# Seven-product FFN blocks: two partial sums copied into PSUM by ScalarE, products in the order 1 5 6 2 7 3 4, weight operands rounded two at a time

## The chip, the cores and the metric

The kernel runs on one core of a Trainium2 chip. The metric is the device time of one execution in microseconds (us), the median of several runs. The core's engines are TensorE (PE in the profile; PEld is its weight load), VectorE (DVE), ScalarE (ACT), GpSimd (POOL) and SyncE (SP, which issues the DMA transfers here). Each engine runs its own queue of instructions in order; semaphores tie the queues together. SBUF is the on-chip memory of 128 partitions; PSUM is the memory into which TensorE accumulates, in banks of 128 x 512 float32.

## The reference

One layer of a hybrid backbone over 512 latent tokens and 128 context tokens, 640 in all: a modulated RMSNorm, a mixer (attention beside a short convolution), a gated residual, and then the feed-forward network (FFN), which is the part that matters here:

```python
h2 = _rms(x, norm_ffn) * (1 + sc2) + sh2
gate, up = jnp.split(h2 @ w_gate_up, 2, axis=-1)      # 1024 -> 2 x 2816
x = x + g2 * ((jax.nn.silu(gate) * up) @ w_down)      # 2816 -> 1024
```

Everything is float32. The kernel gets float32 accuracy out of TensorE by splitting each operand into a rounded high part and a low part, and by three matmuls for each product (high by high, high by low, low by high).

## The kernel before, in words

**Phases.** The mixer takes the first part of the span. From about 318 us on the kernel computes the FFN. Its 2816 columns are cut into 22 blocks f of 128, in four groups (`GCUT` = 0, 6, 12, 17, 22). After each group, `down` multiplies the finished blocks by their rows of `w_down` and adds into the residual.

**A block.** For block f the operands are the columns of gate (raw tile g, 1024 x 128, two halves A11 and A12 of the 1024 rows) and of up (raw tile u, halves A21 and A22); on the token side they are B11, B12, B21, B22, the two halves of the 1024 features by two halves of the 640 tokens (`LO`, `HI`, 320 each). Blocks 0 and 1 (`NPLAIN` = 2) do the eight half products plainly (`plain`). Blocks 2 to 21 use seven products in place of eight, in the manner of Strassen and Winograd: sums S1 to S4 of the weight halves (VectorE, `op_load` L190 on, the sums at L206) and sums T1 to T4 of the token quarters, computed once (`b_sums` L1060 and L1073). One product (`prod`) is four steps of 128 rows, each with three matmuls of 128 x 320 (`mm3`, L154 to L157): twelve matmuls.

**Products and what joins them.** TensorE's queue is written out by hand, in this order for a block before: P1 = A11 B11 into bank b1 (`ff_a`); P5 = S1 T1 into b3 (`ff_c`); the end of the block before (`ff_end`: VectorE and ScalarE only); P6 = S2 T2 onto b1 (`ff_d`); P2 = A12 B21 into b2 (`ff_b`); and in `ff_e` P7 = S3 T3 onto b1, P4 = A22 T4 into b4, P3 = S4 B22 onto b3. Between them ScalarE copies b1 to SBUF three times (`copy_of` L1187, the copy itself at L1191), as p1 after P1, u2 after P6 and u3 after P7, since the next product goes on adding into the same bank. VectorE adds: b2 + p1 (L1204), then ScalarE's SiLU (L1205); b3 + u3 into cu HI (L1220), which reads b3 before P3 goes on into it; b4 + u3 into cu LO and the product with the SiLU; and in `ff_end` b3 + u2, SiLU (L1231), product (L1232). `ff_out` splits the result into gT, 128 x 640, high part on ScalarE and low part on VectorE.

**Weights.** SP issues the loads (L224), 512 KB for each raw tile, into a ring of three raw tiles (`WFB` = 3). A raw tile is free again when the last sum or rounding that reads it is done. `split` (L150 to L152) makes a rounded operand: ScalarE copies the source into the high part, VectorE subtracts that from the source for the low part. Before, each half (A11, S1, S2, A12, S3, A22, S4) is one such operand of 128 x 512, and its high and low part share one tile; the tiles `wh` and `wl`, four of each, are used in turn. `W` and `plan` keep a list of loads and operands and issue them ahead of their use, `AOP` entries ahead for the FFN.

**What sets the order.** VectorE and ScalarE get their instructions by a scheduler with priorities: `early(n)` raises what it encloses (`SOP` for the operands, `CPP` for the copies, `GSP` for gT's split). While blocks 0 and 1 run, VectorE's order is written out by hand as well, with the low parts of the first weights, the token sums and then the weights of block 2. PSUM in the FFN has six banks for the products and for `down` and two for the rest.

Of the kernel before, what the change touches and what calls it, by code (L numbers as in the profile page):

```python
# [9 lines left out]
F32 = mybir.dt.float32  # L10
F32R = mybir.dt.float32r
AF = mybir.ActivationFunctionType
ALU = mybir.AluOpType
AX = mybir.AxisListType

P = 128
# [4 lines left out]
TOK = NT * P  # L21
# [7 lines left out]
HALF = TOK // 2  # L29
# [23 lines left out]
CPP = 50  # L53
GSP = 30
FEND = 2
AOP = 9
NPLAIN = 2
PPO = ''
RSP = 0
# [4 lines left out]
SPO = 0  # L64
# [18 lines left out]
WHB = 4  # L83
# [8 lines left out]
def build(ctx, tc, x_prompt, x_sample, c, cache_k, cache_v, c_ctx, norm_mix, norm_ffn, w_ada, b_ada,  # L92
# [3 lines left out]
    act, dve, pool, pe, sp = nc.scalar, nc.vector, nc.gpsimd, nc.tensor, nc.sync  # L96
# [4 lines left out]
    def open_pool(name, side, names):  # L101
        g = tc.tile_pool(name=name, bufs=1, side=side, reuse_waits="tile")
        pools[name] = (g, g.__enter__())
        for n in names.split():
            where[n] = name
# [14 lines left out]
    def T(tag, shape, dt=F32, bufs=1):  # L120
        seq[0] += 1
        return pools[where.get(tag, "A")][1].tile(list(shape), dt, tag=tag, bufs=bufs, name=f"{tag}_{seq[0]}")

    def PB(shape=(P, 512), dt=F32, tag="t"):
        seq[0] += 1
        if kept.get(tag):
            w = kept[tag].pop()
            n = 1
            for y in shape[1:]:
                n *= y  # L130
            w = w[:, :n] if tag != "s" else w
            if tag != "s" and len(shape) > 2:
                names = "abc"[:len(shape) - 1]
                w = w.rearrange("p (" + " ".join(names) + ") -> p " + " ".join(names), **dict(zip(names, shape[1:])))
            return w
        return pools["psum"][1].tile(list(shape), dt, tag=tag, bufs=pbufs[tag], name=f"p{tag}_{seq[0]}")
# [7 lines left out]
    def f32(ap):  # L144
        return ap.bitcast(F32)

    def early(n):
        return tc.high_priority(n)

    def split(hi, lo, src):  # L150
        act.activation(hi, src, AF.Copy)  # L151
        dve.tensor_tensor(lo, src, f32(hi), ALU.subtract)  # L152

    def mm3(out, lh, ll, rh, rl, start, stop, more=False):  # L154
        pe.matmul(out, lh, rh, start=start, stop=False, skip_group_check=more)  # L155
        pe.matmul(out, lh, rl, start=False, stop=False, skip_group_check=more)  # L156
        pe.matmul(out, ll, rh, start=False, stop=stop, skip_group_check=more)  # L157
# [34 lines left out]
    ops = [0]  # L192

    def op_load(e):

        f, name = e[0][1:]
        g, u = (order[place[x, f]][5] for x in "gu")
        a11, a12, a21, a22 = g[:, 0:4], g[:, 4:8], u[:, 0:4], u[:, 4:8]
        if name[0] == "S":
            if name == "S1":  # L200
                sums[f] = T("sx", (P, 2, 4, P), F32, 2)
            s13, s24 = sums[f][:, 0], sums[f][:, 1]
            src, x, y, op = {"S1": (s13, a21, a22, ALU.add), "S2": (s24, s13, a11, ALU.subtract),
                             "S3": (s13, a11, a21, ALU.subtract), "S4": (s24, a12, s24, ALU.subtract)}[name]
            with early(SOP[f >= NPLAIN]):
                (pool if f < SPO else dve).tensor_tensor(src, x, y, op)  # L206
        else:
            src = {"A11": a11, "A12": a12, "A21": a21, "A22": a22}[name]
        w = T(("wh", "wl")[ops[0] % 2], (P, 2, 4, P), F32R, WHB)
        ops[0] += 1  # L210
        with early(SOP[f >= NPLAIN]):
            split(w[:, 0], w[:, 1], src)
        e[5] = w

    sums = {}

# [34 lines left out]
    def load_next(later=False):  # L251
        load(order[stream_at[0]], later)
        stream_at[0] += 1

    def W(key):
        p = place[key]
        while not in_pre[0] and stream_at[0] < len(order):
            nxt = order[stream_at[0]][0][0]
            ahead = AO if nxt == "o" else AOP if nxt in ("g", "u", "op") else AHEAD
            if stream_at[0] > p + ahead or order[stream_at[0]][2] > phase[0]:  # L260
                break
            load_next()
        assert order[p][5] is not None, key
        return order[p][5]
# [19 lines left out]
            plan(("ada", 5, j, kp), wa[:, 2 * kp:2 * kp + 2, 5 * D + j * 512:5 * D + (j + 1) * 512], 2, "f")  # L284

    GROUPS = [list(range(a, b)) for a, b in zip(GCUT, GCUT[1:])]
    PLAIN, PRODS = ("A11", "A12", "A21", "A22"), ("A11", "S1", "S2", "A12", "S3", "A22", "S4")

    def plan_raw(f, x, ph=3):
        col = f * P + (DFF if x == "u" else 0)  # L290
# [297 lines left out]
    for x in P1SEQ.split():  # L588
        k = int(x[1:] if x[0] == "d" else x[1:2] or 0)
# [306 lines left out]
    cu = {}  # L896
# [89 lines left out]
    LO, HI = slice(0, HALF), slice(HALF, TOK)  # L986
# [55 lines left out]
    B = {}  # L1042
# [35 lines left out]
    for j in range(2):  # L1078
        cols = slice(j * 512, (j + 1) * 512)
        for n, t in enumerate(TORD):  # L1080
# [8 lines left out]
            for half in range(2):  # L1089
                for p in range(4):  # L1090
                    wh, wl = W(("o", j, 2 * half + p // 2))
# [22 lines left out]
            with early(XP[j]):  # L1114
                m = T("mix", (P, 512), F32, 2)
                if j == 0:
                    act.activation(m, ab[0], AF.Copy, scale=rA[t])
                    dve.scalar_tensor_tensor(m, ab[1], rB[t], m, ALU.mult, ALU.add)
                    e = pool if n < PX else dve
# [28 lines left out]
    close_pool("D")  # L1148
    close_pool("F")
    open_pool("Y2", "left", "B22 T1 T2 T3 T4")  # L1150
    open_pool("G", "right", "cg cu p1 u2 u3 dm tr")
    gT, st, pair = {}, {}, [None]

    def FB():
        return PB((P, 512), tag="f")

    def prod(out, f, a, b, start=True, stop=True, more=False):
        w = W(("op", f, a))
        for k in range(4):
            mm3(out[:, :HALF], w[:, 0, k], w[:, 1, k], *B[b][k], start and k == 0, stop and k == 3, more)  # L1160

    def plain(f, bs, toks, mid=None):

# [24 lines left out]
    def copy_of(tag, ps):  # L1188
        x = T(tag, (P, HALF))
        with early(CPP):  # L1190
            act.activation(x, ps[:, :HALF], AF.Copy)  # L1191
        return x

    def ff_a(f):
        b1 = FB()
        prod(b1, f, "A11", "B11")
        cg = T("cg", (P, TOK), F32, 2)
        st[f] = [b1, copy_of("p1", b1), cg, None, None, None, None]

    def ff_b(f):  # L1200
        b2 = FB()
        prod(b2, f, "A12", "B21")
        b1, p1, cg = st[f][0:3]
        dve.tensor_tensor(cg[:, LO], b2[:, :HALF], p1, ALU.add)  # L1204
        act.activation(cg[:, LO], cg[:, LO], AF.Silu)  # L1205

    def ff_c(f):
        st[f][3] = FB()
        prod(st[f][3], f, "S1", "T1")

    def ff_d(f):
        prod(st[f][0], f, "S2", "T2", start=False, more=True)
        st[f][4] = copy_of("u2", st[f][0])

    def ff_e(f):
        b1, _, cg, b3, u2 = st[f][0:5]
        prod(b1, f, "S3", "T3", start=False, more=True)
        u3 = copy_of("u3", b1)
        cu = T("cu", (P, TOK), F32, 2)
        dve.tensor_tensor(cu[:, HI], b3[:, :HALF], u3, ALU.add)  # L1220
        b4 = FB()
        prod(b4, f, "A22", "T4")
        dve.tensor_tensor(cu[:, LO], b4[:, :HALF], u3, ALU.add)
        dve.tensor_tensor(cu[:, LO], cu[:, LO], cg[:, LO], ALU.mult)
        prod(b3, f, "S4", "B22", start=False, more=True)
        st[f] = cg, cu, b3, u2

    def ff_end(f):
# [46 lines left out]
    for gi, grp in enumerate(GROUPS):  # L1275
        for f in grp:
            if f == 0:
                dve_order = tc.manual_schedule(engines={mybir.EngineType.DVE})
                dve_order.__enter__()
                b_plain("B12 B22", slice(0, 192))  # L1280
                for x in range(NPLAIN):
                    plain(x, ("B11", "B21"), LO, None if x else lambda: h2_turn(TORD[-1], BPL))
                    if x == 0:
                        with early(BPL):
                            b_plain("B12 B22", slice(192, HALF))
                        b_sums(slice(128, HALF))
                        for _ in range(4):
                            load_next()
                b_sums(slice(0, 128))
                dve_order.__exit__(None, None, None)  # L1290
                phase[0] = 3
                for x in range(NPLAIN):
                    plain(x, ("B12", "B22"), HI)
            elif f >= NPLAIN:
                ff_a(f)
                if f - 1 in st and FEND == 1:
                    ff_end(f - 1)
                ff_c(f)
                if f - 1 in st:
                    ff_end(f - 1)  # L1300
                ff_d(f)
                ff_b(f)
                ff_e(f)
                if f == grp[-1] or FEND == 0:
                    ff_end(f)
# [6 lines left out]


tile_hymba = with_exitstack(build)

_INS = ["x_prompt", "x_sample", "c", "cache_k", "cache_v", "c_ctx", "norm_mix", "norm_ffn", "w_ada", "b_ada",
# [44 lines left out]
```

## Time and profile before

| | |
|---|---|
| timed runs | 757.63, 758.66, 758.73 us; median 758.66 us |
| profiled execution, its span | 755.2 us; no other time is shown for it, and the median of the runs is 3.5 us above this span |
| TensorE busy | 737.5 us, 98% of the span, 4618 matmuls |
| VectorE busy | 551.7 us, 73% |
| ScalarE busy | 378.8 us, 50% |
| DMA | 84.52 MB, mean 112 GB/s |
| granted TensorE clock | 0.999 |

The span runs from the first to the last recorded instruction of one profiled execution; the timed runs are other executions. A line of the timeline is: start in us, length in us, engine, line of the kernel, operation, output tile <- input tiles (buffer numbers left out), shapes, count, and in brackets how long the engine stood idle before it and what it waited for. Instructions on one engine overlap a little at their ends, so what an instruction costs its engine is read from start to start.

### The profile page before, as it was taken

The page shows a single profiled execution, that of the slowest core. Times are in us where ns is not written, and L with a number is a line of the kernel's source. Part 1 is how long each engine was busy: PE and PEld are TensorE (multiplying, and loading weights), DVE is VectorE, ACT ScalarE, POOL GpSimd, SP SyncE. Part 2 cuts the span into 40 slices and gives each one's busy share as a digit, 9 for nine tenths or more (in the row PEclk, how much of TensorE's full clock was granted, in tenths as well). Part 3 has the DMA queues.
Part 4 walks back from the last instruction along what each step waited for, and adds up shares of the span by engine and source line. Part 5 has one row for each costly group of instructions (what it writes and reads, how often), then busy time and mean ns, then how long its engine had stood idle before and what let it go on. Part 6 is the DMA issues. An engine that isn't in the chain of part 4 may idle for free.

```text
span 755.2 us, 11953 instructions
## 1 busy us (share of the span) xinstructions
PE 737.5 (98%) x4618; PEld 665.2 (88%) x4618; DVE 551.7 (73%) x997; ACT 378.8 (50%) x745; POOL 42.6 (6%) x75
## 2 busy tenths in 40 slices
PE   7999899999999999999999999999999999999997
PEld 5678888988998887899998799998889998899986
DVE  5558877666666798779979778884678866788653
ACT  5356777667656534765552235553125541255410
POOL 2403101011000110100000000000000000000000
PEclk9999999999999999999999999999999999999999
DMA  9985133532432464031235313133113232222312
GB/s 290 294 236 163 51 104 102 165 92 91 159 107 91 133 224 138 1 112 54 81 118 157 108 58 110 58 111 112 56 56 104 67 112 78 62 86 84 112 56 83
DMA packets 101389, 84.52 MB, mean 112 GB/s; under 512 B 3502, under 2 KB 81650, under 8 KB 101332
## 3 DMA queue, kind: packets, MB, share of 16 engines
q1 hardware_dynamic: 100980, 83.39, 35.9%
q8 instruction: 36, 0.59, 0.3%
q0 software_dynamic: 352, 0.37, 0.3%
q14 instruction: 21, 0.17, 0.1%
HBM read 79.68 MB, written 2.75 MB: 109 GB/s over the span
## 4 chain that ended last, share of the span: by engine, by line
PE 83%; DVE 7%; ACT 5%; DMA 2%; issue 1%; SPq 1%; POOL 0%; ACTq 0%
PE pf L155 17%; PE pf L157 17%; PE pf L156 17%; PE pc L710 3%; PE pc L712 3%; PE pc L711 3%; PE po L868 3%; PE ps L824 2%; PE ph L155 2%; PE ph L157 2%; PE ph L156 2%; PE pc L388 2%; PE pt L851 2%; DMA wf<-in_w_in_dram 1%; PE ps L155 1%
## 5 line engine op out<-in xcount | busy, mean ns | idle before, releaser
L151 ACT ACTIVATE wh<-wf 128x512 fp32r<-128x512 f32 (+1 forms) x68 | 55.5, 816 | 81.1 <-PE pf L157 59.3
L155 PE MATMUL pf<-wh,gT 128*128 128x512 f32 (+1 forms) x225 | 86.9, 386 | 0.0
L156 PE MATMUL pf<-wl,gT 128*128 128x512 f32 (+1 forms) x225 | 86.5, 385 | 0.0
L157 PE MATMUL pf<-wh,gT 128*128 128x512 f32 (+1 forms) x225 | 86.5, 384 | 0.0
L710 PE MATMUL pc<-hH,wh 128*128 128x320 f32 x192 | 61.1, 318 | 0.0
L712 PE MATMUL pc<-hH,wl 128*128 128x320 f32 x192 | 59.3, 309 | 0.0
L711 PE MATMUL pc<-hL,wh 128*128 128x320 f32 x192 | 59.3, 309 | 0.0
L152 DVE TENSOR_TENSOR wl<-wf,wh 128x1024 fp32r<-128x1024 f32 (+1 forms) x34 | 39.4, 1160 | 25.2 <-ACT wh L151 22.1
L155 PE MATMUL pf<-T,wh 128*128 128x320 f32 x160 | 49.6, 310 | 0.5 <-ACT u L1191 0.5
L156 PEld LDWEIGHTS pf<-wl,gT 128*128 128x128 f32 x225 | 42.3, 188 | 8.6 <-issue 0.2
L155 PEld LDWEIGHTS pf<-wh,gT 128*128 128x128 f32 x225 | 42.3, 188 | 8.6 <-issue 0.2
L157 PEld LDWEIGHTS pf<-wh,gT 128*128 128x128 f32 x225 | 42.3, 188 | 8.3
L156 PE MATMUL pf<-T,wh 128*128 128x320 f32 x160 | 49.4, 309 | 0.0
L155 PE MATMUL pf<-T,wl 128*128 128x320 f32 x160 | 49.4, 309 | 0.0
L156 PE MATMUL pf<-T,wl 128*128 128x320 f32 x160 | 49.4, 309 | 0.0
L157 PE MATMUL pf<-T,wl 128*128 128x320 f32 x160 | 49.4, 309 | 0.0
L157 PE MATMUL pf<-T,wh 128*128 128x320 f32 x160 | 49.4, 309 | 0.0
L155 PE MATMUL pf<-B,wl 128*128 128x320 f32 x152 | 47.1, 310 | 0.0
L157 PE MATMUL pf<-B,wl 128*128 128x320 f32 x152 | 47.0, 309 | 0.0
L156 PE MATMUL pf<-B,wl 128*128 128x320 f32 x152 | 47.0, 309 | 0.0
L155 PE MATMUL pf<-B,wh 128*128 128x320 f32 x136 | 42.2, 310 | 1.5 <-DVE cu L1220 1.5
L151 ACT ACTIVATE wl<-wf 128x512 fp32r<-128x512 f32 x34 | 21.2, 625 | 41.6 <-PE pf L156 34.8
(306 smaller groups left out, 2058.7 us busy)
## 6 DMA issues: line engine op xcount, KB each, us to landing
wf<-in_w_gate_up_dram SPq DMA_DIRECT2D x44, 512.0 KB, 4.0
aw<-in_w_ada_dram SPq DMA_DIRECT2D x24, 512.0 KB, 4.1
wf<-in_w_down_dram SPq DMA_DIRECT2D x20, 512.0 KB, 3.3
wf<-in_w_in_dram SPq DMA_DIRECT2D x18, 512.0 KB, 5.5
af<-in_w_ada_dram SPq DMA_DIRECT2D x32, 256.0 KB, 6.4
x<-in_x_sample_dram SPq DMA_DIRECT2D x8, 512.0 KB, 6.2
wf<-in_w_out_dram SPq DMA_DIRECT2D x8, 512.0 KB, 4.4
wf<-in_w_ada_dram SPq DMA_DIRECT2D x8, 512.0 KB, 3.7
```

The lines of the kernel that those rows point to most:

```text
L151: act.activation(hi, src, AF.Copy)
L152: dve.tensor_tensor(lo, src, f32(hi), ALU.subtract)
L155: pe.matmul(out, lh, rh, start=start, stop=False, skip_group_check=more)
L156: pe.matmul(out, lh, rl, start=False, stop=False, skip_group_check=more)
L157: pe.matmul(out, ll, rh, start=False, stop=stop, skip_group_check=more)
L388: pe.matmul(out[CG * g:CG * (g + 1)], cp[:, k], w, start=(k < 4), stop=(k >= KD - 4), skip_group_check=True)
L710: pe.matmul(acc, wh[:, k], hH[k][:, c0:c0 + n], start=(k == 0), stop=False)
L711: pe.matmul(acc, wh[:, k], hL[k][:, c0:c0 + n], start=False, stop=False)
L712: pe.matmul(acc, wl[:, k], hH[k][:, c0:c0 + n], start=False, stop=(k == KD - 1))
L824: pe.matmul(s2[:, g, :320], q, kk[:, v, P + g * 320:P + (g + 1) * 320], start=(i == 0), stop=(i == 1))
L851: pe.transpose(tp[:, i, h], u[3][h][:, kt * P:(kt + 1) * P], ident)
L868: pe.matmul(ov, w, x[:, i].rearrange("p a q -> p (a q)"), start=(g == 0 and i == 0 and n == 0), stop=(last and i == len(kts) - 1 and n == 1))
```

## The change

In the blocks of seven products, three things are different.

- After P1 ScalarE copies b1 into the PSUM bank b2, and P2 accumulates on it; after P7 it copies b1 into the bank b4, and P4 accumulates on that. The copies p1 and u3 in SBUF, and the two additions on VectorE that used them for the `LO` half, are gone. SiLU reads b2, and the product for cu LO reads b4 straight from PSUM.
- The last three products run as P7, P3, P4 in place of P7, P4, P3. A new copy p5 of b3 is taken to SBUF after P5; cu HI is then b1 + p5 and no longer reads b3.
- Operands are rounded two at a time: A11 with A12, A21 with A22 in the plain blocks, S1 with S2, S3 with S4; one tile `wh` of 128 x 1024 is the high part of both, one tile `wl` the low part. A22 of the seven-product blocks is still rounded alone. `AOP` is 6 in place of 9.

```diff
-AOP = 9
+AOP = 6
@@ op_load
-            if name == "S1":
-                sums[f] = T("sx", (P, 2, 4, P), F32, 2)
-            s13, s24 = sums[f][:, 0], sums[f][:, 1]
-            src, x, y, op = {"S1": (s13, a21, a22, ALU.add), "S2": (s24, s13, a11, ALU.subtract),
-                             "S3": (s13, a11, a21, ALU.subtract), "S4": (s24, a12, s24, ALU.subtract)}[name]
+            if name == "S12":
+                sums[f] = T("sx", (P, 8, P), F32, 2)
+            s13, s24 = sums[f][:, 0:4], sums[f][:, 4:8]
             with early(SOP[f >= NPLAIN]):
-                (pool if f < SPO else dve).tensor_tensor(src, x, y, op)
+                for out, x, y, op in {"S12": ((s13, a21, a22, ALU.add), (s24, s13, a11, ALU.subtract)),
+                                      "S34": ((s13, a11, a21, ALU.subtract), (s24, a12, s24, ALU.subtract))}[name]:
+                    dve.tensor_tensor(out, x, y, op)
+            src = sums[f]
         else:
-            src = {"A11": a11, "A12": a12, "A21": a21, "A22": a22}[name]
-        w = T(("wh", "wl")[ops[0] % 2], (P, 2, 4, P), F32R, WHB)
-        ops[0] += 1
+            src = {"A1": g, "A2": u, "A22": a22}[name]
+        if name == "A22":
+            w = T(("wh", "wl")[ops[0] % 2], (P, 2, 4, P), F32R, WHB)
+            ops[0] += 1
+            e[5] = w[:, 0], w[:, 1]
+        else:
+            e[5] = T("wh", (P, 8, P), F32R, WHB), T("wl", (P, 8, P), F32R, WHB)
         with early(SOP[f >= NPLAIN]):
-            split(w[:, 0], w[:, 1], src)
-        e[5] = w
+            split(*e[5], src)
...
-    PLAIN, PRODS = ("A11", "A12", "A21", "A22"), ("A11", "S1", "S2", "A12", "S3", "A22", "S4")
+    PLAIN, PRODS = ("A1", "A2"), ("A1", "S12", "S34", "A22")
+    PAIRS = {"A11": ("A1", 0), "A12": ("A1", 4), "A21": ("A2", 0), "A22": ("A2", 4),
+             "S1": ("S12", 0), "S2": ("S12", 4), "S3": ("S34", 0), "S4": ("S34", 4)}
@@ prod
-        w = W(("op", f, a))
+        x, k0 = PAIRS[a] if f < NPLAIN or a != "A22" else (a, 0)
+        wh, wl = W(("op", f, x))
         for k in range(4):
-            mm3(out[:, :HALF], w[:, 0, k], w[:, 1, k], *B[b][k], start and k == 0, stop and k == 3, more)
+            mm3(out[:, :HALF], wh[:, k0 + k], wl[:, k0 + k], *B[b][k], start and k == 0, stop and k == 3, more)
@@ ff_a
-        b1 = FB()
+        b1, b2 = FB(), FB()
         prod(b1, f, "A11", "B11")
-        cg = T("cg", (P, TOK), F32, 2)
-        st[f] = [b1, copy_of("p1", b1), cg, None, None, None, None]
+        with early(CPP):
+            act.activation(b2[:, :HALF], b1[:, :HALF], AF.Copy)
+        st[f] = [b1, b2, T("cg", (P, TOK), F32, 2), None, None, None]
@@ ff_b
-        prod(b2, f, "A12", "B21")
-        dve.tensor_tensor(cg[:, LO], b2[:, :HALF], p1, ALU.add)
-        act.activation(cg[:, LO], cg[:, LO], AF.Silu)
+        prod(b2, f, "A12", "B21", start=False, more=True)
+        act.activation(cg[:, LO], b2[:, :HALF], AF.Silu)
@@ ff_c
-        prod(st[f][3], f, "S1", "T1")
+        prod(b3, f, "S1", "T1")
+        st[f][4] = copy_of("p5", b3)
@@ ff_e
         prod(b1, f, "S3", "T3", start=False, more=True)
-        u3 = copy_of("u3", b1)
+        b4 = FB()
+        with early(CPP):
+            act.activation(b4[:, :HALF], b1[:, :HALF], AF.Copy)
         cu = T("cu", (P, TOK), F32, 2)
-        dve.tensor_tensor(cu[:, HI], b3[:, :HALF], u3, ALU.add)
-        b4 = FB()
-        prod(b4, f, "A22", "T4")
-        dve.tensor_tensor(cu[:, LO], b4[:, :HALF], u3, ALU.add)
-        dve.tensor_tensor(cu[:, LO], cu[:, LO], cg[:, LO], ALU.mult)
+        dve.tensor_tensor(cu[:, HI], b1[:, :HALF], p5, ALU.add)
         prod(b3, f, "S4", "B22", start=False, more=True)
+        prod(b4, f, "A22", "T4", start=False, more=True)
+        dve.tensor_tensor(cu[:, LO], b4[:, :HALF], cg[:, LO], ALU.mult)
```

More of the change, by code (lines that the diff above doesn't have):

```diff
@@ L1150, in build @@
     open_pool("Y2", "left", "B22 T1 T2 T3 T4")
-    open_pool("G", "right", "cg cu p1 u2 u3 dm tr")
+    open_pool("G", "right", "cg cu p5 u2 dm tr")
     gT, st, pair = {}, {}, [None]
@@ L1194, in ff_a @@
     def ff_a(f):
-        b1 = FB()
+        b1, b2 = FB(), FB()
         prod(b1, f, "A11", "B11")
-        cg = T("cg", (P, TOK), F32, 2)
-        st[f] = [b1, copy_of("p1", b1), cg, None, None, None, None]
+        with early(CPP):
+            act.activation(b2[:, :HALF], b1[:, :HALF], AF.Copy)
+        st[f] = [b1, b2, T("cg", (P, TOK), F32, 2), None, None, None]
     def ff_b(f):
-        b2 = FB()
-        prod(b2, f, "A12", "B21")
-        b1, p1, cg = st[f][0:3]
-        dve.tensor_tensor(cg[:, LO], b2[:, :HALF], p1, ALU.add)
-        act.activation(cg[:, LO], cg[:, LO], AF.Silu)
+        b2, cg = st[f][1:3]
+        prod(b2, f, "A12", "B21", start=False, more=True)
+        act.activation(cg[:, LO], b2[:, :HALF], AF.Silu)
     def ff_c(f):
-        st[f][3] = FB()
-        prod(st[f][3], f, "S1", "T1")
+        b3 = st[f][3] = FB()
+        prod(b3, f, "S1", "T1")
+        st[f][4] = copy_of("p5", b3)
     def ff_d(f):
         prod(st[f][0], f, "S2", "T2", start=False, more=True)
-        st[f][4] = copy_of("u2", st[f][0])
+        st[f][5] = copy_of("u2", st[f][0])
     def ff_e(f):
-        b1, _, cg, b3, u2 = st[f][0:5]
+        b1, _, cg, b3, p5, u2 = st[f]
         prod(b1, f, "S3", "T3", start=False, more=True)
-        u3 = copy_of("u3", b1)
+        b4 = FB()
+        with early(CPP):
+            act.activation(b4[:, :HALF], b1[:, :HALF], AF.Copy)
         cu = T("cu", (P, TOK), F32, 2)
-        dve.tensor_tensor(cu[:, HI], b3[:, :HALF], u3, ALU.add)
-        b4 = FB()
-        prod(b4, f, "A22", "T4")
-        dve.tensor_tensor(cu[:, LO], b4[:, :HALF], u3, ALU.add)
-        dve.tensor_tensor(cu[:, LO], cu[:, LO], cg[:, LO], ALU.mult)
+        dve.tensor_tensor(cu[:, HI], b1[:, :HALF], p5, ALU.add)
         prod(b3, f, "S4", "B22", start=False, more=True)
+        prod(b4, f, "A22", "T4", start=False, more=True)
+        dve.tensor_tensor(cu[:, LO], b4[:, :HALF], cg[:, LO], ALU.mult)
         st[f] = cg, cu, b3, u2
```

## The prediction, made before the result was known

> **What bounds the kernel now.** I read the page first, then the granted clock, the waits of TensorE in the FFN part, its busy time by stretch, and last the timeline of the stretch that stood out.
>
> ```profile
> span 755.2 us, 11953 instructions
> PE 737.5 (98%) x4618; PEld 665.2 (88%) x4618; DVE 551.7 (73%) x997; ACT 378.8 (50%) x745; POOL 42.6 (6%) x75
> PE 83%; DVE 7%; ACT 5%; DMA 2%; issue 1%; SPq 1%; POOL 0%; ACTq 0%
> core 0: 755.2 us, clock 0.999
> PE pf L155 <- DVE cu L1220: 1.5, 1, 1.5
> PE pf L155 <- ACT u L1191: 0.5, 1, 0.5
> ```
>
> TensorE is busy 98% of the span at a clock of 0.999, and the change leaves its number of matmuls as it was. Up to about 318 us the two programs have the same order on every engine, so only the FFN can differ. The last two lines are the waits of TensorE between 330 and 755 us (total, count, mean): two, worth 2 us. Where are they?
>
> ```profile
> 350.00:377.00 27.00, 25.00 (x168) 24.32 (x167) 26.04 (x47) 15.79 (x30) 0.00 (x0) 1.00 0.30 87
> 377.00:402.00 25.00, 25.00 (x172) 25.00 (x171) 19.92 (x32) 12.90 (x22) 0.00 (x0) 1.00 0.40 128
> ```
>
> Busy time by stretch: length, then PE, PEld, DVE, ACT, POOL, granted clock, DMA. In 350 to 377 us (blocks f=2 and f=3, the first of seven products) VectorE is full, 26.04 of 27 us, and TensorE stands 2 us; in the next 25 us TensorE is full and VectorE has 5 us to spare. TensorE's timeline gives the exact loss:
>
> ```profile
> 350.05 0.31 PE L155 MATMUL pf<-B,wh 128*128 128x320 f32 x1
> 357.93 0.41 PE L155 MATMUL pf<-T,wh 128*128 128x320 f32 x1 [0.52 <-ACT u L1191]
> 363.19 0.41 PE L155 MATMUL pf<-B,wh 128*128 128x320 f32 x1 [1.48 <-DVE cu L1220]
> 377.37 0.31 PE L155 MATMUL pf<-B,wh 128*128 128x320 f32 x1
> ...
> 502.64 0.31 PE L155 MATMUL pf<-T,wl 128*128 128x320 f32 x1
> 504.40 0.31 PE L155 MATMUL pf<-B,wh 128*128 128x320 f32 x1
> 516.58 0.31 PE L157 MATMUL pf<-T,wh 128*128 128x320 f32 x1
> 516.90 0.41 PE L155 MATMUL pf<-B,wl 128*128 128x320 f32 x1
> ```
>
> Undisturbed, a product of twelve matmuls takes 504.40 − 502.64 = 1.76 us start to start (0.147 each), a block of seven 12.32. From P1 of f=2 (350.05) to P1 of f=4 (377.37) it is 27.32 us for 14 × 1.76 = 24.64: 2.68 lost. P7 is 0.84 late (357.93 against 350.05 + 4 × 1.76 = 357.09), P3 another 1.74 (363.19 against 357.93 + 3.52), the rest is restarts. One more place, f=11, takes 0.32 over one matmul step and 0.1 for restarting: 0.27 lost. So 2.95 us is all that a change of the order can win: that is the floor, 755.7 from the median of 758.66.
>
> **The change, part by part.** The matmuls stay at twelve a product. The prices:
>
> ```profile
> 344.48 0.68 DVE L206 TENSOR_TENSOR sx<-wf 128x512 f32<-128x512 f32 x1
> 345.08 0.48 DVE L1174 TENSOR_TENSOR cu<-pf,cg 128x320 f32<-128x320 f32 x1
> 345.48 0.68 DVE L206 TENSOR_TENSOR sx<-sx,wf 128x512 f32<-128x512 f32 x1
> 357.90 0.82 DVE L152 TENSOR_TENSOR gT<-cu,gT 128x640 fp32r<-128x640 f32 x1
> 358.64 0.69 DVE L206 TENSOR_TENSOR sx<-wf 128x512 f32<-128x512 f32 x1
> 414.56 1.22 DVE L152 TENSOR_TENSOR wl<-wf,wh 128x1024 fp32r<-128x1024 f32 x1
> 415.70 0.68 DVE L1270 TENSOR_TENSOR dm<-pf,g 128x512 f32<-128x512 f32 x1
> 389.93 1.06 ACT L151 ACTIVATE wh<-wf 128x1024 fp32r<-128x1024 f32 x1 [1.12 <-PE pf L157]
> 390.90 0.46 ACT L1231 ACTIVATE cg<-cg 128x320 f32<-128x320 f32 x1
> L151 ACT ACTIVATE wh<-sx 128x512 fp32r<-128x512 f32 x40 | 25.1, 627 | 14.8 <-PE pf L157 5.9 <-ACT wl L151 4.9 <-DVE sx L206 3.9
> L1191 ACT ACTIVATE u<-pf 128x320 f32<-128x320 f32 x40 | 17.4, 436 | 30.4 <-PE pf L157 30.4
> 357.46 0.42 ACT L1191 ACTIVATE u<-pf 128x320 f32<-128x320 f32 x1
> ```
>
> Start to start, VectorE takes 0.60 us for 512 columns, 0.40 for 320, 0.74 for 640 and 1.14 for 1024. ScalarE takes 1.06 for a rounding of 1024 columns alone, 0.97 with work behind it (390.90 − 389.93), and 0.44 for a copy of 320.
>
> *Arithmetic.* VectorE does, in a block before, four sums and seven narrow low parts (11 × 0.60), six operations on 320 columns (2.40) and one gT low part (0.74): 9.74 us. After, four sums and one narrow part (3.00), three wide low parts (3.42), four on 320 (1.60) and gT: 8.76. So 0.98 less in a block of 12.32. ScalarE keeps four copies and two SiLU and does three wide roundings and one narrow one in place of seven narrow: less too. Under a TensorE that is full both are worth nothing; they count only in f=2 and f=3, where VectorE is late.
>
> *P3 no longer waits for VectorE.* P3 goes on into b3. Before, the addition cu HI (L1220) had to read b3 first; after, p5 has been copied out two products earlier. The 1.74 in f=2 and the 0.27 in f=11 lose their cause. What is late next in f=2 is ScalarE's copies behind VectorE's backlog, so I walk the start.
>
> *The start, f=2 and f=3.* The raw tiles come from a ring of three; what frees them is the last reading on VectorE.
>
> ```profile
> 322.24 0.68 DVE L152 TENSOR_TENSOR wl<-wf,wl 128x512 fp32r<-128x512 f32 x1
> 326.89 0.63 ACT L151 ACTIVATE wh<-wf 128x512 fp32r<-128x512 f32 x1 [0.54 <-DMA wf<-in_w_gate_up_dram]
> 343.87 0.69 DVE L152 TENSOR_TENSOR wh<-wf,wh 128x512 fp32r<-128x512 f32 x1
> 363.65 0.69 DVE L152 TENSOR_TENSOR wh<-wf,wh 128x512 fp32r<-128x512 f32 x1
> 368.31 0.69 DVE L206 TENSOR_TENSOR sx<-wf 128x512 f32<-128x512 f32 x1 [0.66 <-DMA wf<-in_w_gate_up_dram]
> ```
>
> The narrow part that ends at 322.92 frees a tile for u of f=1; one wide part does it some 1.6 us earlier, so ScalarE's idle 0.54 ahead of 326.89 goes and its two roundings become one (0.07 less). I take 0.6 us for the token sums T1 to T4 behind it, with 0 and 0.9 as ends. VectorE then comes to the weights of f=2 at 343.3 in place of 343.87. In the built order: low part of A1 1.14, a sum 0.6, an operation on 320 0.4, a sum 0.6, to 346.0; ScalarE rounds S1 and S2 together to 347.1; VectorE does their low part to 348.2, then 0.4, three of 0.6 with gT's 0.74 and two more of 0.6 to the sums S3 and S4, to 352.4; ScalarE rounds them to 353.5, and only then copies b1 into b2, to 354.0. P6 accumulates on b1 and needs that copy. Its turn is 350.05 + 3.52 = 353.57: **0.45 late**. VectorE goes on with 0.4, 0.6, 0.6, 1.14, 0.6, 0.6 to 356.4, where the token sum T4 is ready; ScalarE copies it (0.54), rounds A1 of f=3 (0.97) and then copies u2 (0.44): 358.4. P7's turn is 354.05 + 3.52 = 357.57: **0.85 late**. In f=3: P7 of f=2 ends at 360.2, ScalarE copies b1 into b4 (0.44) and rounds S1 and S2 of f=3 (1.06), VectorE does the low part (1.14), an addition (0.4) and the two sums that free g's tile (1.2), together 364.5. The next load needs 3.97 us (from 363.65 + 0.69 to 368.31 in the rows above), then come two sums (1.2), the rounding (0.97) and u2 (0.44), with four hand-overs of 0.05 (357.46 + 0.42 to 357.93): 371.3, against P7's turn at 358.45 + 12.32 = 370.77, and I take **0.75 late** with the restarts. Together 2.05, with a restart after f=2 2.15, against 2.68 before: −0.53. With the token sums not earlier at all, the copies that P6 and P7 wait for move with them and the gain is nearly gone (−0.1); with 0.9 earlier it is −1.0 in all.
>
> *A copy into PSUM.* No row of before shows ScalarE writing PSUM. By ScalarE's slope into SBUF, (1060 − 627)/512 × 320 = 0.27 us with nothing for the start of an instruction is the low end, a whole 512-column rounding (0.63) the high end. I take 0.44, the copy of the same 320 columns. The ends move only P6 of f=2, by 0.2 either way.
>
> *The steady blocks, f=4 to f=21.* The wait to fear is P7's for u2. Ahead of u2 ScalarE now has a wide rounding of the next block's A1, which may start only when P6 has read the weight tile to its next-to-last matmul: 0.05 after P2's start, then 0.97, u2 0.44 and hand-over 0.05, 1.51 us of P2's 1.76. **Spare 0.25**. The copy of b1 into b4 has P3's 1.76 for 0.44, the copy into b2 P5's: over 1 us each. A raw tile is freed some 2.4 us after P7's start (a low part behind P2's end, 1.14, and two sums, 1.2), 3.7 earlier than in f=3 above (364.5 − 358.45 = 6.1), which leaves the loads 2.9 us. Cost 0; beyond 0.25 the cover is gone. The queues of SP and POOL keep their order; the look-ahead of 6 entries in place of 9 is one block either way (two loads and four or seven operands): 0. The down products between the groups get no new wait: 0.
>
> Here a rule speaks against the change. In these rows a narrow rounding at 0.52 in place of 0.97 ahead of u2 would bring u2 0.45 earlier. The Trainium skill, Perfetto Trace Analysis, section "Optimizing Scalar/DVE Operations", says that grouping work into larger operations pays where the engine is saturated, and that where it is not but still makes bubbles elsewhere, smaller instructions let work finish sooner. By it, with ScalarE at 50%, P7's stall in f=2 and f=3 would each be about 0.45 shorter with narrow roundings; the trace agrees with its first half only for VectorE in 350 to 377 us.
>
> The sum: −0.53 − 0.27 = **−0.8 us**, 755.2 to 754.4 in the span. The three runs shown are 757.63, 758.66 and 758.73, about 3.5 us above the profiled span, so on the median: **757.9**.
>
> **The rivals.** *B, faster: the start's stalls go.* VectorE has 0.98 less per block, P3 waits for nothing; if the token sums come 0.9 earlier and the scheduler's order leaves the copies ahead of roundings in time, most of 2.95 goes: 755.7 to 757. For it: the backlog of 26.04 in 27 us is what is cut. Against: in the built order the copies stand behind wide roundings.
>
> *A, slower: the spare of 0.25 ahead of u2 isn't there.* It decides at one point: rounding, copy and hand-overs above P2's 1.76. Each 0.1 beyond costs 0.1 and a restart of 0.1 in each of 18 blocks; missed by 0.15, that is 18 × 0.25 = 4.5, less 0.8: 762.4. For it: this row, where the rounding starts 0.19 after the next product's start, not 0.05.
>
> ```profile
> 375.61 0.31 PE L155 MATMUL pf<-B,wl 128*128 128x320 f32 x1
> 375.80 0.63 ACT L151 ACTIVATE wh<-sx 128x512 fp32r<-128x512 f32 x1 [0.80 <-PE pf L157]
> ```
>
> There the last matmul of the product releases it (L157); after, the high parts' tile is released one matmul (0.147) before. Even at 0.19 the sum is 1.65, under 1.76. A smaller form of it, a start that is worse by 1 to 2 us, is in the same chance.
>
> **How the numbers follow.** I call 0.2% (1.5 us) no change; the three runs span that much. Forecast 0.47, its own range 756.9 to 758.9 (of it 0.04 below 757.1); B 0.28; A 0.25. Faster 0.32, same 0.43, slower 0.25. The range leaves out 0.05 of B at the low end and 0.15 of A: 755.9 to 760.6.
>
> **What would show it.** TensorE's waits after 350 us on ScalarE's copies (P6, P7 of f=2, P7 of f=3) of 0.4 to 0.9 each, none on cu; from 377 us on none at all; VectorE near 24 in 350 to 377. Eighteen small waits on u2 would make A; none between 350 and 377 would make B. A copy into PSUM far from 0.44, or loads that wait in the steady blocks, would break the walk.

## The result

The changed kernel takes 757.07 us (median of 20 runs, 756.28 to 758.02) against 758.41 for the kernel before (20 runs, 757.49 to 759.82): ratio 0.9983, 95% interval 0.9977 to 0.9990. That is 1.3 us less, with an interval of 0.8 to 1.7, and 1.3 falls within the 0.2% (1.5 us) that the prediction called no change, though the interval reaches a little beyond it. The forecast had been 0.8 less.

### The profile page after: what moved, and what is told of

It reads as the page before. It is cut to its first block, busy times and chain, and to the rows that moved or that the text cites. A ratio compares the mean times of both kernels' runs of the same rounds, so it can differ in the third digit from the quotient of the medians.

```text
span 755.8 us, 11732 instructions
## 1 busy us (share of the span) xinstructions
PE 738.3 (98%) x4618; PEld 666.0 (88%) x4618; DVE 527.1 (70%) x893; ACT 374.9 (50%) x701; POOL 42.4 (6%) x75
## 4 chain that ended last, share of the span: by engine, by line
PE 85%; DVE 5%; ACT 4%; DMA 3%; issue 1%; SPq 1%; POOL 0%; ACTq 0%
PE pf L155 17%; PE pf L157 17%; PE pf L156 17%; PE pc L716 3%; PE pc L718 3%; PE pc L717 3%; PE ph L155 2%; PE ph L157 2%; PE ph L156 2%; PE po L874 2%; PE ps L830 2%; PE pt L857 2%; PE pc L394 2%; DMA af<-in_w_ada_dram 2%; ACT wh L151 1%; DVE wl L152 1%
## 5 line engine op out<-in xcount | busy, mean ns | idle before, releaser
L151 ACT ACTIVATE wh<-wf 128x1024 fp32r<-128x1024 f32 (+1 forms) x68 | 65.6, 968 | 86.0 <-PE pf L157 50.2
L155 PE MATMUL pf<-B,wh 128*128 128x320 f32 x288 | 89.1, 309 | 0.0
L157 PE MATMUL pf<-B,wl 128*128 128x320 f32 x288 | 89.1, 309 | 0.0
L156 PE MATMUL pf<-B,wh 128*128 128x320 f32 x288 | 89.0, 309 | 0.0
L157 PE MATMUL pf<-T,wl 128*128 128x320 f32 x280 | 86.5, 309 | 0.0
L151 ACT ACTIVATE wh<-sx 128x1024 fp32r<-128x1024 f32 x40 | 42.4, 1061 | 80.1 <-PE pf L157 38.9
L152 DVE TENSOR_TENSOR wl<-sx,wh 128x1024 fp32r<-128x1024 f32 x40 | 48.9, 1224 | 26.8 <-ACT wh L151 23.1
L157 PEld LDWEIGHTS pf<-B,wl 128*128 128x128 f32 x288 | 54.1, 188 | 0.1
L155 PEld LDWEIGHTS pf<-B,wh 128*128 128x128 f32 x288 | 54.1, 188 | 0.1
L156 PEld LDWEIGHTS pf<-B,wh 128*128 128x128 f32 x288 | 54.1, 188 | 0.1
L155 PEld LDWEIGHTS pf<-T,wh 128*128 128x128 f32 x280 | 52.6, 188 | 1.8 <-ACT u L1198 1.8
L156 PEld LDWEIGHTS pf<-T,wh 128*128 128x128 f32 x280 | 52.6, 188 | 0.0
L157 PEld LDWEIGHTS pf<-T,wl 128*128 128x128 f32 x280 | 52.6, 188 | 0.0
```

## The profile after

The page of the changed kernel:

```profile
span 755.8 us, 11732 instructions
PE 738.3 (98%) x4618; PEld 666.0 (88%) x4618; DVE 527.1 (70%) x893; ACT 374.9 (50%) x701; POOL 42.4 (6%) x75
```

TensorE's waits from 318 us on (total, count, longest), and below them busy time by stretch for the two stretches shown of before:

```profile
PE pf L155 <- ACT u L1198: 1.3, 2, 0.6
```

```profile
350.00:377.00 27.00, 25.73 (x174) 25.20 (x174) 24.62 (x37) 16.70 (x28) 0.00 (x0) 1.00 0.28 83
377.00:402.00 25.00, 25.00 (x172) 25.00 (x172) 17.52 (x26) 12.08 (x21) 0.00 (x0) 1.00 0.37 112
```

VectorE has 24.6 us less to do over the span (551.7 to 527.1), and of that at most 1.3 us shows in the time: TensorE, busy for 98% of the span, was the bound. The waits on cu are gone; two waits on the copy u2 are left. The profiled span is 0.6 longer than that of before, and this would mislead: the difference arises ahead of the FFN. The first matmul of the FFN, before and after:

```profile
320.89 0.39 PE L155 MATMUL pf<-B,wh 128*128 128x320 f32 x1
```

```profile
322.61 0.39 PE L155 MATMUL pf<-B,wh 128*128 128x320 f32 x1
```

It comes 1.72 later, and the 1.72 is there already at the first instruction in which the two differ, a rounding on ScalarE (at 317.90 before and 319.61 after). The last matmul, before and after:

```profile
750.92 0.28 PE L157 MATMUL pf<-wh,gT 128*128 128x256 f32 x1
```

```profile
751.58 0.28 PE L157 MATMUL pf<-wh,gT 128*128 128x256 f32 x1
```

From the first to the last it is 430.03 us before and 428.97 after: 1.06 less. This length of the FFN is what I compare from here on; beside it stand the timed ratios.

TensorE's timeline has the two stalls that are left, and ScalarE's shows what stood ahead of u2:

```profile
351.87 0.31 PE L155 MATMUL pf<-B,wh 128*128 128x320 f32 x1
358.77 0.31 PE L157 MATMUL pf<-B,wl 128*128 128x320 f32 x1
359.71 0.41 PE L155 MATMUL pf<-T,wh 128*128 128x320 f32 x1 [0.63 <-ACT u L1198]
371.98 0.31 PE L157 MATMUL pf<-B,wl 128*128 128x320 f32 x1
372.93 0.41 PE L155 MATMUL pf<-T,wh 128*128 128x320 f32 x1 [0.64 <-ACT u L1198]
501.82 0.31 PE L155 MATMUL pf<-T,wh 128*128 128x320 f32 x1
```

```profile
354.78 0.42 ACT L1205 ACTIVATE pf<-pf 128x320 f32<-128x320 f32 x1
355.13 0.72 ACT L151 ACTIVATE gT<-cu 128x640 fp32r<-128x640 f32 x1
...
357.75 0.63 ACT L1065 ACTIVATE T<-tr 128x512 fp32r<-128x512 f32 x1 [0.54 <-DVE tr L1079]
358.29 1.04 ACT L151 ACTIVATE wh<-wf 128x1024 fp32r<-128x1024 f32 x1
359.24 0.41 ACT L1198 ACTIVATE u<-pf 128x320 f32<-128x320 f32 x1
...
371.49 1.06 ACT L151 ACTIVATE wh<-sx 128x1024 fp32r<-128x1024 f32 x1 [1.41 <-DVE sx L206]
372.46 0.42 ACT L1198 ACTIVATE u<-pf 128x320 f32<-128x320 f32 x1
...
500.16 1.06 ACT L151 ACTIVATE wh<-wf 128x1024 fp32r<-128x1024 f32 x1 [1.17 <-PE pf L156]
501.12 0.42 ACT L1198 ACTIVATE u<-pf 128x320 f32<-128x320 f32 x1
```

P7 starts 0.94 after the start of P2's last matmul (0.95 in f=3), where 0.147 is the undisturbed step: 0.79 late in f=2 and 0.80 in f=3. After each stall comes what I call a restart: the first matmul takes 0.41 in place of 0.31, and the next starts 0.1 later than it would. Together that is 1.8 us, where before had 2.95. In both blocks a wide rounding of 1.0 us stands in ScalarE's queue right ahead of u2. In a steady block the same pair ends at 501.54 and P7 starts at 501.82.

## The experiments

Theory: the gain is the lost waits of P3 and an earlier start; what is left is u2's place in ScalarE's queue behind a wide rounding. Rivals: the copies into PSUM, which unload VectorE, make the gain; or the wide roundings make it.

**1. The changed kernel with narrow roundings.**

```diff
-    PLAIN, PRODS = ("A1", "A2"), ("A1", "S12", "S34", "A22")
+    PLAIN, PRODS = ("A11", "A12", "A21", "A22"), ("A11", "S1", "S2", "A12", "S3", "A22", "S4")
-AOP = 6
+AOP = 9
```

(with `op_load` and `prod` as before the change)

> The changed kernel with the roundings of before (each half an operand of 512 columns, look-ahead 9), so that only the PSUM copies, p5 and the order 7 3 4 are left of the change. Theory 1 (the wide roundings help only by the start: in the changed kernel the token sums of T start 1.2 us earlier against TensorE): T is 1.2 us later, P6 of f=2 is late by about 0.4, P7 of f=2 and f=3 by 0.5 to 1; TensorE loses about 2.4 us in f=2 and f=3, 0.6 more than the changed kernel's 1.8; time about 0.6 us above it. Theory 2 (the rule on smaller instructions): u2 comes 0.45 earlier in both blocks, TensorE loses about 0.9, time about 0.9 us under the changed kernel.

Ratio to the kernel before 0.9981 (0.9973 to 0.9989), 1.4 us less; the FFN takes 428.59. The waits on u2:

```profile
PE pf L155 <- ACT u L1191: 0.8, 2, 0.5
```

Neither theory had the size. P7 is late by 0.69 and 0.44, between the two; P6 is hardly late (0.01 and a restart), though the token sums start as late as in the kernel before (12.0 after the first FFN matmul). The wide roundings are not what makes the gain: without them it is the same within the intervals.

**2. The kernel before with the wide roundings alone.** The edit is the reverse of the one above, put into the kernel before.

> The kernel before with the wide roundings and the look-ahead of 6 alone; products 1 5 6 2 7 4 3 and the SBUF copies stay. Theory 1: the token sums come 1.2 us earlier, but P3 still waits for the addition cu HI on VectorE: of P3's 1.74 in f=2 about 0.7 is left, P7 of f=2 and f=3 wait 0.5 to 0.8 behind wide roundings; TensorE loses 1.8 to 2.5; time 0.4 to 1.1 under the kernel before. Theory 2 (the products' order and the PSUM copies make the gain): P3 keeps about 1.7, time as before within 0.3.

Ratio 1.0082 (1.0069 to 1.0095): 6.2 us *slower*, which neither theory expected. TensorE's waits, then VectorE in one of the steady blocks:

```profile
PE pf L155 <- DVE cu L1227: 5.5, 9, 1.7
```

```profile
505.51 1.23 DVE L152 TENSOR_TENSOR wl<-sx,wh 128x1024 fp32r<-128x1024 f32 x1
506.78 0.69 DVE L206 TENSOR_TENSOR sx<-wf,wf 128x512 f32<-128x512 f32 x1
507.38 0.68 DVE L206 TENSOR_TENSOR sx<-wf,sx 128x512 f32<-128x512 f32 x1
507.99 0.48 DVE L1227 TENSOR_TENSOR cu<-pf,u 128x320 f32<-128x320 f32 x1
```

u3 is ready at 506.83 in this block, but the addition cu HI stands behind a wide low part and two sums and starts at 507.99. P3 waits for it, 0.63 and a restart in eight blocks and 1.86 in f=3; in six more blocks it is 0.03 late and pays a restart. I had looked for VectorE's backlog only in f=2 and f=3; a wider instruction ahead of an addition that TensorE waits for makes a wait in blocks where VectorE has much time to spare on average (it is busy for 71% of the span here).

**3. Wide roundings in the two plain blocks alone**, in the kernel before.

```diff
+        if name in ("A1", "A2"):
+            e[5] = T("wh", (P, 8, P), F32R, WHB), T("wl", (P, 8, P), F32R, WHB)
+            with early(SOP[0]):
+                split(*e[5], order[place["g" if name == "A1" else "u", f]][5])
+            return
-    PLAIN, PRODS = ("A11", "A12", "A21", "A22"), ...
+    PLAIN, PRODS = ("A1", "A2"), ...
```

(`prod` takes the halves of a plain block out of the pair; the look-ahead stays at 9)

> The kernel before with wide roundings in the two plain blocks alone. Theory 1: the raw tile is freed earlier, the token sums start about 1.2 us earlier against TensorE, and VectorE's addition ahead of P3 of f=2 with them: P3's 1.74 falls to about 0.6, P7's 0.67 to about 0.2; time about 1.4 under the kernel before. Theory 2: the start has nothing to do with it; 0.

Ratio 0.9988 (0.9979 to 0.9996), 0.9 less; FFN 429.03, 1.0 less. The token sums start 11.0 us after the first FFN matmul in place of 12.0. P7 of f=2 no longer waits; P3 still does:

```profile
PE pf L155 <- DVE cu L1230: 1.1, 1, 1.1
```

P3's delay (1.74 in the prediction, of which 0.1 is P7's restart) falls from 1.64 to 1.26, not to 0.6. From P1 of f=2 on, TensorE loses 1.64 in place of 2.95, close to the 1.4 less that was expected, though with another share for P3 and P7; but the plain blocks ahead of it (from the first FFN matmul on) take 29.48 us in place of 29.16, which no run explains. So the earlier start is real and worth about 1 us to the old product order, less than expected.

**4. The changed kernel, ScalarE's wide roundings in halves.**

```diff
-            split(*e[5], src)
+            if f < NPLAIN or name == "A22":
+                split(*e[5], src)
+            else:
+                hi, lo = e[5]
+                act.activation(hi[:, 0:4], src[:, 0:4], AF.Copy)
+                act.activation(hi[:, 4:8], src[:, 4:8], AF.Copy)
+                dve.tensor_tensor(lo, src, f32(hi), ALU.subtract)
```

> The changed kernel with ScalarE's wide roundings of the seven-product blocks cut into two of 512 columns; VectorE's low parts stay wide. The copy u2 can go between the halves. If the wide rounding ahead of u2 is what holds P7 of f=2 and f=3: P7's 0.79 and 0.80 fall by 0.45 each, to about 0.35; time 0.9 under the changed kernel; in the steady blocks u2 ends about 0.7 ahead of P7 in place of 0.28. If VectorE's backlog holds them: no change within 0.2.

755.03 us, ratio 0.9964 (0.9951 to 0.9977): 2.7 less than the kernel before, about 1.4 less than the changed kernel; FFN 427.23. No wait of TensorE is left in the seven-product blocks. Here u2 goes between the halves:

```profile
356.41 0.62 ACT L221 ACTIVATE wh<-wf 128x512 fp32r<-128x512 f32 x1
356.97 0.63 ACT L1071 ACTIVATE T<-tr 128x512 fp32r<-128x512 f32 x1
357.50 0.42 ACT L1204 ACTIVATE u<-pf 128x320 f32<-128x320 f32 x1
357.82 0.62 ACT L222 ACTIVATE wh<-wf 128x512 fp32r<-128x512 f32 x1
```

The stalls went altogether, not by 0.45 each: the scheduler also put T4's copy and u2 in a better order. This is the floor that the prediction gave, 2.95 less, reached within the interval (1.7 to 3.7 less), and a kernel that beats both.

**5. The products in the old order, 7 4 3.**

```diff
-        prod(b3, f, "S4", "B22", start=False, more=True)
         prod(b4, f, "A22", "T4", start=False, more=True)
         dve.tensor_tensor(cu[:, LO], b4[:, :HALF], cg[:, LO], ALU.mult)
+        prod(b3, f, "S4", "B22", start=False, more=True)
```

> The changed kernel with its last three products in the old order, 7 4 3. If P4 has to wait for ScalarE's copy of b1 into its bank: hand-over 0.05, copy 0.42, hand-over 0.05 and restart 0.1, about 0.6 in each of 20 blocks: 12 us above the changed kernel, about 769, with 20 waits of P4's first matmul on the copy. If the copy into PSUM is hidden in any case, so that the order does not matter: no change within 0.3.

Ratio 1.0196 (1.0182 to 1.0210): 14.9 slower than the kernel before, 16 slower than the changed one. TensorE's waits, then one of the 20 in TensorE's timeline and in ScalarE's:

```profile
PE pf L155 <- ACT pf L1227: 10.3, 20, 0.6
```

```profile
388.85 0.31 PE L157 MATMUL pf<-T,wl 128*128 128x320 f32 x1
389.67 0.41 PE L155 MATMUL pf<-T,wh 128*128 128x320 f32 x1 [0.51 <-ACT pf L1227]
```

```profile
389.20 0.42 ACT L1227 ACTIVATE pf<-pf 128x320 f32<-128x320 f32 x1 [0.52 <-PE pf L157]
```

Each costs 0.67 and a restart of 0.1. My 0.6 left out that a wait for a product is a wait for its last matmul's end (0.31 after its start), where the next matmul would have started at 0.147. So the copy into b4 needs the new order.

**6. u2 copied twice.**

```diff
-            act.activation(x, ps[:, :HALF], AF.Copy)
+            for _ in range(1 + (tag == "u2")):
+                act.activation(x, ps[:, :HALF], AF.Copy)
```

> The changed kernel with the copy u2 made twice over, the second over the first. Measures what lies beyond the spare that ScalarE has ahead of P7 (0.28 less a hand-over of 0.05 in the profile of the changed kernel). If that spare is as small as it looks: a copy takes 0.36 to 0.44, so P7 is late by 0.13 to 0.21 and a restart of 0.1 in each of 18 blocks, and by a whole copy in f=2 and f=3: 4.9 to 6.4 us above the changed kernel, 20 waits on u. If ScalarE has more to spare than that: under 1 us, in f=2 and f=3 alone.

Ratio 1.0085 (1.0071 to 1.0099), about 7.7 above the changed kernel; the FFN is 7.2 longer. In a steady block:

```profile
502.89 1.06 ACT L151 ACTIVATE wh<-wf 128x1024 fp32r<-128x1024 f32 x1 [1.18 <-PE pf L156]
503.85 0.89 ACT L1199 ACTIVATE u<-pf 128x320 f32<-128x320 f32 x2
```

P7 is 0.20 to 0.25 late there, with a restart of 0.1, and by 1.28 and 1.55 in f=2 and f=3, 0.49 and 0.75 more than in the changed kernel. Eighteen times 0.30 to 0.35 and these 1.24 make 6.6 to 7.5, above what was expected: the second copy starts 0.45 after the first, not 0.36, and f=3 loses more than one copy. The spare is as small as it looked: one copy more uses it up in every block, and 0.45 less the spare of 0.23 is the 0.22 that P7 is late.

**7. The order 7 3 4 and p5 alone**, in the kernel before.

```diff
-    PLAIN, PRODS = ..., ("A11", "S1", "S2", "A12", "S3", "A22", "S4")
+    PLAIN, PRODS = ..., ("A11", "S1", "S2", "A12", "S3", "S4", "A22")
...
+        st[f][5] = copy_of("p5", st[f][3])
...
-        dve.tensor_tensor(cu[:, HI], b3[:, :HALF], u3, ALU.add)
+        dve.tensor_tensor(cu[:, HI], b1[:, :HALF], p5, ALU.add)
+        prod(b3, f, "S4", "B22", start=False, more=True)
         b4 = FB()
         prod(b4, f, "A22", "T4")
         dve.tensor_tensor(cu[:, LO], b4[:, :HALF], u3, ALU.add)
         dve.tensor_tensor(cu[:, LO], cu[:, LO], cg[:, LO], ALU.mult)
-        prod(b3, f, "S4", "B22", start=False, more=True)
```

> The kernel before with p5 and the order 7 3 4 alone (cu HI is b1 + p5): no copy into PSUM, p1 and u3 stay in SBUF with their two additions on VectorE, roundings narrow, look-ahead 9. Theory 1 (the gain of the narrow kernel comes from P3's wait): P3's 1.74 and the 0.27 of f=11 go, P7 of f=2 and f=3 wait about 0.7 and 0.4 as in the narrow kernel; time 1.4 to 1.8 under the kernel before. Theory 2 (VectorE's 0.8 us less per block, which only the PSUM copies give, is needed): P7's waits grow by about 0.8 in f=3; time within 0.8 of the kernel before.

Ratio 1.0007 (0.9998 to 1.0016): no gain. The waits on cu are gone, others came, in blocks where I expected none:

```profile
PE pf L155 <- ACT p L1191: 1.6, 4, 0.6
```

```profile
484.85 0.74 ACT L151 ACTIVATE gT<-cu 128x640 fp32r<-128x640 f32 x1 [1.44 <-DVE cu L1226]
485.49 0.42 ACT L1191 ACTIVATE p<-pf 128x320 f32<-128x320 f32 x1
```

P6 waits for p1. In three of the four blocks p1 stands behind gT's rounding, which waits for VectorE's last operation on cu; in f=2 it stands behind a rounding of weights. Theory 1 fails for this kernel. Theory 2 has the outcome, and its place (P7 of f=3) is wrong.

**8. Wide roundings with the order 7 3 4 and p5, still no copy into PSUM**: the edits of 2 and 7 together.

> The kernel with wide roundings alone, which took 5.7 us more, given p5 and the order 7 3 4; still no copy into PSUM. Theory 1 (what cost it was P3 waiting for cu HI behind a wide low part and two sums on VectorE): the nine waits on cu go, and the time falls to that of the changed kernel, 1 to 1.7 under the kernel before. Theory 2 (VectorE is too full without the PSUM copies): waits move to P7 or to the operands in the steady blocks, 2 to 6 us above the kernel before.

755.57 us, ratio 0.9968 (0.9955 to 0.9981), 2.4 less than the kernel before; FFN 427.57. TensorE is late at one place, P7 of f=2, by 0.30 and a restart. ScalarE around u2 of f=2 and of f=3:

```profile
355.80 1.06 ACT L151 ACTIVATE wh<-wf 128x1024 fp32r<-128x1024 f32 x1
356.76 0.62 ACT L1065 ACTIVATE T<-tr 128x512 fp32r<-128x512 f32 x1
357.28 0.42 ACT L1198 ACTIVATE u<-pf 128x320 f32<-128x320 f32 x1
...
368.85 0.43 ACT L1198 ACTIVATE u<-pf 128x320 f32<-128x320 f32 x1
...
371.96 1.06 ACT L151 ACTIVATE wh<-sx 128x1024 fp32r<-128x1024 f32 x1 [0.19 <-DVE sx L206]
```

The wide roundings are there, but in f=2 that of A1 comes ahead of T4's copy, and in f=3 that of S1 and S2 comes behind u2. So what cost 6.2 us in run 2 was P3's wait, and the copies into PSUM are not needed for the gain. This kernel differs from the changed one only by those copies and the additions that go with them. It has 15.4 us more for VectorE to do (542.5 against 527.1), and yet its FFN is 1.4 us shorter; the intervals of the two timed ratios overlap. By the traces, then, the first of the three parts of the change brought nothing beside the other two.

**9. A look-ahead of 4 in the changed kernel.**

```diff
-AOP = 6
+AOP = 4
```

> The changed kernel with a look-ahead of 4 entries in place of 6. The instructions are the same; in ScalarE's queue the rounding of S1 and S2 of f=4 now stands behind u2 of f=3, and the rounding of A1 of f=3 ahead of the copy of T4. If it is the place of u2 in ScalarE's queue that holds P7, and not the amount of work: P7's waits in f=2 and f=3 (0.79 and 0.80, with restarts 1.8 together) fall to under 0.6 together, and the time to 1.2 to 1.8 under the changed kernel, with no instruction made smaller. If VectorE's backlog or the size of the roundings holds it: the waits stay at 1.4 or more. Should the shorter look-ahead bring the raw loads too late, waits on the operands would show in the steady blocks.

Ratio 0.9981 (0.9972 to 0.9989); FFN 428.22, 0.75 less than the changed kernel's. In the timings the two cannot be told apart, and 1.2 was expected. In the trace P7 of f=3 does not wait; P7 of f=2 is late by 0.59 and a restart of 0.1, just above what was expected; two small waits, of P6 in f=4 and P7 in f=5, cost another 0.35 with their restarts. ScalarE and then TensorE:

```profile
357.03 0.63 ACT L1065 ACTIVATE T<-tr 128x512 fp32r<-128x512 f32 x1 [0.17 <-DVE tr L1079]
357.57 0.42 ACT L1198 ACTIVATE u<-pf 128x320 f32<-128x320 f32 x1
```

```profile
358.04 0.42 PE L155 MATMUL pf<-T,wh 128*128 128x320 f32 x1 [0.42 <-ACT u L1198]
```

With the same instructions the wait of f=3 is gone, so that one was a matter of place in the queue. In f=2 u2 still waits for T4's copy, which waits for VectorE (0.17): there the backlog has a share.

**All runs beside each other.** FFN is the time from its first to its last matmul in the profile; "timed" is the ratio of the runs times the kernel before's median on the same chip.

| kernel | FFN, us | against before | timed against before |
|---|---|---|---|
| before | 430.03 | | |
| the change | 428.97 | −1.1 | −1.3 |
| 1 narrow | 428.59 | −1.4 | −1.4 |
| 2 wide roundings alone | 436.38 | +6.4 | +6.2 |
| 3 wide in the plain blocks | 429.03 | −1.0 | −0.9 |
| 4 halves on ScalarE | 427.23 | −2.8 | −2.7 |
| 5 order 7 4 3 | 444.83 | +14.8 | +14.9 |
| 6 u2 twice | 436.16 | +6.1 | +6.4 |
| 7 order and p5 alone | 430.30 | +0.3 | +0.5 |
| 8 wide and order | 427.57 | −2.5 | −2.4 |
| 9 look-ahead 4 | 428.22 | −1.8 | −1.4 |

The length of the FFN agrees with every timed difference within 0.4 us, and the stalls of TensorE make up most of these differences: from P1 of f=2 on, 2.95 are lost before, 1.8 after, and under 0.1 in run 4.

Runs 1, 7, 8 and the change itself have the order 7 3 4 and p5 in common. By the traces, the copies into PSUM are worth 1.7 us with narrow roundings (run 7 to run 1, where the last two operands of the list change places as well) and cost 1.4 with wide ones (run 8 to the change). By the rows shown it hangs on what order the scheduler then gives ScalarE's copies and roundings; no run shows that by itself.

## Why the prediction was right

- *The floor.* 2.95 us to be won and no more. Run 4 has no wait left in the seven-product blocks and gains 2.7 (1.7 to 3.7).
- *P3.* Its waits on cu (1.74 in f=2, 0.27 in f=11) are gone, as said. (In the lines of waits the third number is the longest wait, not the mean; with a count of one they are the same.) What the text did not see is how much the order carries: with wide roundings and the old order P3 waits in nine blocks (run 2, +6.2). The parts of the change were costed one by one as if they added; −0.8 held because the built change has the new order beside the wide roundings.
- *P6 of f=2, 0.45 late: wrong.* It is not late. The mis-sized term is the earlier start of the token sums, taken as 0.6 with ends of 0 and 0.9. By the rows below (before, then after) it is 12.03 and 10.82 us after the first FFN matmul, 1.21 earlier. The copy into b2 ends at 355.20, 0.19 before P6's turn at 351.87 + 3.52. Already in the kernel before, P6 lost 0.16 there, which the text counts with P7. With P7 as below, that leaves 1.8 us lost where the text had 2.15: 1.1 gained by the trace in place of 0.8. The timed 1.3 does not differ from that beyond its interval (0.8 to 1.7).

```profile
332.92 0.95 DVE L1073 TENSOR_TENSOR tr<-gT 128x768 f32<-128x768 f32 x1
```

```profile
333.43 0.95 DVE L1079 TENSOR_TENSOR tr<-gT 128x768 f32<-128x768 f32 x1
```

- *P7 of f=2 and f=3, 0.85 and 0.75 late.* Measured 0.79 and 0.80, each with 0.1 for the restart. In f=2 the walk was right, T4's copy and then the wide rounding of A1 ahead of u2. In f=3 the rounding that stood there was that of S1 and S2 of f=4, as in the walk. That the two sizes came so close is in part luck. In f=2 the copy and P7's turn both came about half a us earlier than in the walk (u2 ends 7.78 after P1 starts, the walk has 8.35). In f=3 the 0.75 holds 0.2 for restarts, so the walk's own delay was 0.53, and 0.80 was measured. Counted from P1 of f=2, P7 of f=3 starts after 21.06 us, and the walk has 21.25 (371.3 − 350.05): the loss up to there was nearly right as a whole, and what P6 did not lose was in part lost at P7 of f=3 instead.
- *The copy into PSUM, taken as 0.44.* 0.42 in length, and 0.35 from start to start with work behind it (354.78 to 355.13). The means are 421 and 422 ns for the two copies into PSUM and 435 ns for p5 into SBUF, nearly all after an idle stretch: hardly a difference.
- *The spare of 0.25 ahead of u2 in the steady blocks.* 0.28, less a hand-over of 0.05: 0.23, in 18 of 18 blocks. Rival A did not come about; run 6 bears out its price beyond the point. There P7 misses by 0.20 to 0.25 and each block loses 0.30 to 0.35, the miss and a restart of 0.1; the text's 0.25 was the same rule for a miss of 0.15.
- *Rival B*, the stalls of the start gone, is what run 4 does, and run 8 all but 0.4 us of it. The text put the copies behind the wide roundings in the built order, and that is what kept the change from it: in runs 4, 8 and 9 a stall shrinks or goes where the rounding ahead of u2 is halved, comes earlier or comes behind u2.
- *The rule on smaller instructions.* The Trainium skill, Perfetto Trace Analysis, section "Optimizing Scalar/DVE Operations", says that where an engine is not saturated and its work still makes bubbles elsewhere, breaking up instructions may let work finish sooner. Run 4 agrees, with ScalarE busy for half of the span: 1.4 us less than the changed kernel by halving roundings. Run 1, with narrow roundings on both engines, is the case that the prediction worked out from the rule: P7's delays fell by 0.10 and 0.36, not by 0.45 each, and the time did not change clear of noise. Run 8 adds what the rule does not say: with wide roundings kept, and the copies otherwise placed, all but 0.4 us of the bubbles is gone too.

What stays open: whether runs 4 and 8 differ (their intervals overlap), and why the scheduler's order comes out as well as it does in run 8 and worse with the copies into PSUM. No run fixed that order by hand.

## What to carry to other kernels

When one engine is 98% busy, count its stalls first: their sum is the most that a reordering can win, and unloading an engine beside it wins nothing by itself (the change takes 24.6 us off VectorE and gains 1.3; run 8 takes 9.2 off and gains 2.4). Then look, for each copy or addition that the bound engine waits for, at what stands ahead of it in its own queue: a wider instruction there cost 0.7 us in eight of 20 blocks on an engine that was idle for 29% of the span (run 2). Parts of this change that are worth nothing (run 7) or cost 6 us (run 2) alone gain 2.4 together (run 8), so try the pairs and not only the parts.

## What the runs showed that was not expected

- The prediction took the 3.5 us between the profiled span (755.2) and the median for what lies around a span. In the changed kernel's timed runs it is 1.7 to 1.8 (757.61 us for a span of 755.8); at that, by my estimate, the profiled execution of before took 757.0, less than any of its three runs shown. The first FFN matmul of the eleven profiled executions lies between 320.89 and 322.91, although the order of work up to about 318 us is the same before and after. A profiled span alone cannot show a difference of 1 us here; the length of the FFN in the same trace can.
- A first matmul that waits for the product just before it pays 0.31 − 0.147 = 0.16 us for that product's last matmul to end, on top of the copy and the hand-overs (388.85 to 389.67 in run 5).
